# The second MLP product of two of four token chunks in seven block products of eight

## The chip, the core and the metric

The kernel runs on one core of a Trainium2 chip. The metric is the time of one execution on the device in microseconds (us). Five engines work side by side, each through its own list of instructions in a fixed order: TensorE (PE, with its weight loads as PEld), VectorE (DVE), ScalarE (ACT), GpSimd (POOL) and SyncE (SP), which issues nearly all DMAs. They wait for each other through semaphores.

## What is computed

The reference is a trunk of two layers for 1024 tokens of width 1024. What matters here is the MLP at each layer's end, with 4096 inner columns:

```python
def sq_relu_mlp(h, w1, w2):
    a = jax.nn.relu(h @ w1)
    return (a * a) @ w2
...
        h = rms_norm(x, mlp_norm_g[layer])
        x = x + sq_relu_mlp(h, mlp_w1[layer], mlp_w2[layer])
    return rms_norm(x, final_g)
```

Everything is float32.

## The kernel before

The tokens are worked on in two chunks of 512 (x[0] and x[1], each four row blocks of 128 tokens times two column halves of 512). So there are four MLPs: a0 (layer 0, first chunk), b0 (layer 0, second chunk), a1 and b1 (layer 1). In the program they stand in the order a0, b0, a1, b1; the convolution module of layer 1 is woven into b0 and a1, and a0 and b1 run nearly alone. Names in the profile carry the chunk's letter (m_a, o_b), not the layer.

PE multiplies float32 in a form that rounds, so each operand is split in a high and a low part, and each product takes three matmuls: low times high (L157), high times low (L158) and high times high (L159), all 128x128 by 128x512. The high part is made by a cast on ACT, the low part by a subtraction on DVE; for the weights these are wh and wl, made from a loaded tile raw (L104 and L105 for w2, L125 and L126 for w1), 1024 columns at a time.

`mlp` (L243) works on 32 inner tiles of 128 columns. m1(f) multiplies the normed chunk hT by a column tile of w1 in 24 matmuls into a PSUM bank (tag m1, two banks), takes relu to r (L252), squares r twice on ACT, once cast into the high part ah (L254) and once in place (L255), and subtracts for the low part al (L256). m2(g, h) takes four inner tiles (G = 4) and one column half of w2: for each of four row blocks 12 matmuls into a PSUM bank o (tag mm, four banks), and an addition into x on DVE (L240). A list sets the order in which the program is written: the first m1 of the next group stands ahead of the two m2 of a group:

```python
            n = (g + 1) * G
            order += [(m1, n)] if n < NF else []
            order += [(m2, g, 0), (m2, g, 1)]
            order += [(m1, f) for f in range(n + 1, min(n + G, NF))]
```

From what is written a scheduler sets, when the program is built, the order on each engine; at run time it is fixed. Tiles come from pools with a number of buffers for each tag: 48 of [128, 512] in pool hp (x, the normed chunk, and others), four wh and four wl of [128, 1024], two raw. The norm ahead of an MLP (`norm_parts`) squares and sums x on ACT, scales it on DVE, transposes it on PE into the bank pair tr, and makes hh (ACT) and hl (DVE). In a0 the norm of x[1], named m, stands behind the first steps of a0. `finish` does the last norm and the output.

Of the kernel before, what the change touches and what calls it, by code (L numbers as in the profile page):

```python
# [31 lines left out]
def tile_hybrid_trunk(  # L32
# [7 lines left out]
    nc = tc.nc  # L40
# [5 lines left out]
    lp = ctx.enter_context(tc.tile_pool(name="lp", bufs=8))  # L46
# [8 lines left out]
    def hf(name):  # L55
        return ht(name, F32)
# [10 lines left out]
    def m1_ps(name):  # L67
        return mmp[0].tile([P, C], F32, tag="m1", bufs=2, name=name)
# [203 lines left out]
    NG = FF // (G * P)  # L272


    w_in = ev_w_in[0]
    y = [[None] * KT for _ in range(NCH)]
    dp = ctx.enter_context(tc.tile_pool(name="dp", bufs=1, space=bass.MemoryType.DRAM))
    with tc.tile_pool(name="p1", bufs=1) as p1, tc.tile_pool(name="ps1", bufs=1, space=PSUM) as ps1:
        mmp = (ps1, 2)

        def qt(name):
            return p1.tile([P, C], F32R, tag="q", bufs=8, name=name)
# [314 lines left out]
        for h in range(NH):  # L597
            out_proj((1,), 1, h)

    p2 = ctx.enter_context(tc.tile_pool(name="p2", bufs=1))  # L600
    p2.tile([P, 96], F32, tag="pad", bufs=1, name="pad_p2")
    ps2 = ctx.enter_context(tc.tile_pool(name="ps2", bufs=1, space=PSUM))
    mmp = (ps2, 4)

    def bt(name, dt=F32):
        return p2.tile([P, C], dt, tag="b", bufs=11, name=name)

    def ct(name):
        return p2.tile([P, C], F32, tag="c", bufs=9, name=name)


    halo = cp.tile([P, KT, HALO], F32, name="halo")
# [89 lines left out]
        rows_into_x(s[kg * 4:kg * 4 + 4], ws, h, x[c], f"q2{c}{kg}{h}")  # L702

    def finish(c):
        fg = [ct(f"fg{c}{h}") for h in range(NH)]
        for h in range(NH):
            nc.sync.dma_start(fg[h], final_g[h * C:(h + 1) * C].rearrange("(a d) -> a d", a=1).to_broadcast((P, C)))
        for t in range(TT):
            o = [ct(f"fo{c}{t}{h}") for h in range(NH)]
# [24 lines left out]
    steps(a0)  # L734
    b0 = mlp(0, hm[1], x[1], "b0")
    steps(b0, -1)
    h1a = norm(x[0], "od_g", 0, ct, "oa")
# [56 lines left out]
```

## Time and profile before

| what | us |
|---|---|
| median of 3 runs (lowest, highest) | 2218.25 (2216.99, 2218.44) |
| the profiled execution | 2218.34 |
| its span in the trace | 2216.5 |
| PE busy | 2176.4 (98%) |
| DVE busy | 1411.7 (64%) |
| ACT busy | 954.7 (43%) |
| POOL busy | 113.0 (5%) |

The profile is of one execution. Matmuls overlap: each is recorded with about 390 ns, while the next starts some 0.23 us after it, so the starts tell the pace. The granted clock, the share of TensorE's full 2.4 GHz that the chip allows, is 0.997 in the mean. The matmuls of a0 lie between about 518 and 859 us, those of b1 between 1860.7 and 2208.9 us.

### The profile page before, as it was taken

To read this page: it belongs to the slowest core of one execution; us is meant where nothing else is said; L and a number is where in the kernel's file an instruction comes from. 1 tells how busy PE (TensorE), PEld (TensorE's weight loads), DVE (VectorE), ACT (ScalarE), POOL (GpSimd) and SP (SyncE) were. 2 spreads that over 40 slices of the span, in tenths; PEclk is the share of its full clock that TensorE was granted. 3 is DMA by queue.
4 is the path that set the end of the run, shared out by engine and by line. 5 is a ranking of instruction groups with operands and counts; after the bars stand their busy time and mean duration, and the time that the engine had idled before them with its cause. 6 is when DMAs were issued, how large, how long until landed. Compare 5 with 4: busy or idle time off the path is not lost.

```text
span 2216.5 us, 25970 instructions
## 1 busy us (share of the span) xinstructions
PE 2176.4 (98%) x10180; PEld 1768.2 (80%) x10180; DVE 1411.7 (64%) x1934; ACT 954.7 (43%) x1509; POOL 113.0 (5%) x296
## 2 busy tenths in 40 slices
PE   7999999899999999999999999999999999999998
PEld 5867776678888888888888888788888888888887
DVE  4377878856433444579899664999886555444344
ACT  4466677535333334433333362443333545333332
POOL 1000000000000001100000010300000001000000
PEclk9999999999999999999999999999999999999999
DMA  4111013022323223332222323222222224222232
GB/s 160 57 34 43 34 53 127 35 73 67 109 95 95 96 95 100 100 95 95 95 96 96 95 95 96 86 96 95 95 96 95 95 97 147 99 95 95 95 95 76
DMA packets 172010, 199.25 MB, mean 90 GB/s; under 512 B 5648, under 2 KB 120688, under 8 KB 171888
## 3 DMA queue, kind: packets, MB, share of 16 engines
q1 hardware_dynamic: 171872, 197.59, 27.5%
q8 instruction: 80, 1.31, 0.2%
q14 instruction: 42, 0.34, 0.1%
q10 hardware_dynamic: 16, 0.00, 0.0%
HBM read 190.23 MB, written 7.34 MB: 89 GB/s over the span
## 4 chain that ended last, share of the span: by engine, by line
PE 94%; DVE 3%; ACT 1%; DMA 1%; issue 1%; POOL 0%; SPq 0%; DVEq 0%; POOLq 0%; ACTq 0%
PE m_a L157 5%; PE m_a L158 5%; PE m_b L159 5%; PE m_a L159 5%; PE o_a L158 5%; PE o_a L159 5%; PE m_b L157 5%; PE o_a L157 5%; PE m_b L158 5%; PE o_b L159 5%; PE o_b L157 5%; PE o_b L158 5%; PE av L529 2%; PE xg L158 1%; PE wt L521 1%; PE xg L157 1%
## 5 line engine op out<-in xcount | busy, mean ns | idle before, releaser
L648 DVE SCALAR_TENSOR_TENSOR cv<-u,dwT,cv 128x512 f32<-128x512 f32 x480 | 340.3, 756 | 0.2
L157 PE MATMUL o_a<-wh_w2a,al_a 128*128 128x512 f32 x512 | 199.6, 390 | 0.0
L158 PE MATMUL o_a<-wl_w2a,ah_a 128*128 128x512 f32 x512 | 199.5, 390 | 0.0
L157 PE MATMUL o_b<-wh_w2b,al_b 128*128 128x512 f32 x512 | 199.4, 390 | 0.0
L159 PE MATMUL o_b<-wh_w2b,ah_b 128*128 128x512 f32 x512 | 199.4, 389 | 0.0
L158 PE MATMUL o_b<-wl_w2b,ah_b 128*128 128x512 f32 x512 | 199.3, 389 | 0.0
L159 PE MATMUL o_a<-wh_w2a,ah_a 128*128 128x512 f32 x512 | 198.9, 389 | 0.0
L125 ACT CAST wh_w1b<-raw_w1b 128x1024 fp32r<-128x1024 f32 x64 | 67.4, 1053 | 211.8 <-PE o_b L159 168.5
L105 DVE TENSOR_TENSOR wl_w2a<-raw_w2a,wh_w2a 128x1024 fp32r<-128x1024 f32 x64 | 78.3, 1224 | 121.9 <-ACT wh_w2a L104 121.9
L125 ACT CAST wh_w1a<-raw_w1a 128x1024 fp32r<-128x1024 f32 x64 | 67.4, 1054 | 205.2 <-PE o_a L159 169.7
L105 DVE TENSOR_TENSOR wl_w2b<-raw_w2b,wh_w2b 128x1024 fp32r<-128x1024 f32 x64 | 80.3, 1254 | 116.0 <-ACT wh_w2b L104 116.0
L240 DVE TENSOR_TENSOR xr<-o_a,xr 128x512 f32<-128x512 f32 x128 | 87.5, 687 | 75.9 <-PE o_a L159 75.7
L240 DVE TENSOR_TENSOR xr<-o_b,xr 128x512 f32<-128x512 f32 x128 | 87.9, 687 | 71.3 <-PE o_b L159 70.9
L158 PEld LDWEIGHTS o_b<-wl_w2b,ah_b 128*128 128x128 f32 x512 | 96.1, 188 | 19.9
L157 PEld LDWEIGHTS o_a<-wh_w2a,al_a 128*128 128x128 f32 x512 | 96.1, 188 | 19.9
L159 PEld LDWEIGHTS o_b<-wh_w2b,ah_b 128*128 128x128 f32 x512 | 96.1, 188 | 19.8
L159 PEld LDWEIGHTS o_a<-wh_w2a,ah_a 128*128 128x128 f32 x512 | 96.1, 188 | 19.8
L157 PEld LDWEIGHTS o_b<-wh_w2b,al_b 128*128 128x128 f32 x512 | 96.1, 188 | 19.7
L158 PEld LDWEIGHTS o_a<-wl_w2a,ah_a 128*128 128x128 f32 x512 | 96.2, 188 | 19.7
L252 ACT ACTIVATE r_b<-m_b 128x512 f32<-128x512 f32 x64 | 38.3, 599 | 169.6 <-PE m_b L159 169.6
L252 ACT ACTIVATE r_a<-m_a 128x512 f32<-128x512 f32 x64 | 38.3, 598 | 163.0 <-PE m_a L159 163.0
L126 DVE TENSOR_TENSOR wl_w1b<-raw_w1b,wh_w1b 128x1024 fp32r<-128x1024 f32 x64 | 77.9, 1220 | 36.1 <-ACT wh_w1b L125 35.7
(537 smaller groups left out, 5345.0 us busy)
## 6 DMA issues: line engine op xcount, KB each, us to landing
raw_w1a<-in_mlp_w_dram SPq DMA_DIRECT2D x32, 1024.0 KB, 5.1
raw_w2a<-in_mlp_w_dram SPq DMA_DIRECT2D x32, 1024.0 KB, 5.0
raw_w1b<-in_mlp_w_dram SPq DMA_DIRECT2D x32, 1024.0 KB, 5.1
raw_w2b<-in_mlp_w_dram SPq DMA_DIRECT2D x32, 1024.0 KB, 4.9
raw_pw<-in_od_pw_w_dram SPq DMA_DIRECT2D x32, 512.0 KB, 4.5
raw_q<-in_od_pw_w_dram SPq DMA_DIRECT2D x8, 1024.0 KB, 4.9
raw_wo<-in_ev_w_out_dram SPq DMA_DIRECT2D x6, 768.0 KB, 4.9
xa<-in_x_dram SPq DMA_DIRECT2D x16, 256.0 KB, 5.1
```

The source lines that it names most:

```text
L105: paced(V.tensor_tensor(lo, raw, hi.bitcast(F32), op=ALU.subtract), 1)
L125: A.copy(hi, srcs[i])
L126: paced(V.tensor_tensor(lo, srcs[i], hi.bitcast(F32), op=ALU.subtract), 2)
L157: T.matmul(acc, ll, rh, start=(i == 0), stop=False)
L158: T.matmul(acc, lh, rl, start=False, stop=False)
L159: T.matmul(acc, lh, rh, start=False, stop=(i == n - 1))
L240: paced(V.tensor_tensor(xt[t][h], acc, xt[t][h], op=ALU.add), 1.5)
L252: A.activation(r, acc, AF.Relu)
L521: T.transpose(pt[:, b * P:(b + 1) * P], ke[:, b * P:(b + 1) * P], ident)
L529: ins = T.matmul(av[j * 64:j * 64 + 64, tt * P:(tt + 1) * P], vt[lo_s // P + b][:, hc:hc + 64], wts[j][:, b * P:(b + 1) * P], start=(diag ...
L648: waiting.append(lambda k=k, m=m: V.scalar_tensor_tensor(cv[m], u[m][:, k:k + C], dwT[:, k * KT + m:k * KT + m + 1], cv[m], op0=ALU.mult, ...
```

## The change

a0 and b1 are no longer made by `mlp` but by a new function, `mlp7`, in four groups of eight inner tiles; b0 and a1 stay. For the second product it takes the activations as a 2x2 matrix of blocks (rows: the chunk's first and last 256 tokens; columns: even and odd inner tiles), and w2 so too (even and odd inner rows, left and right column half). Strassen's algorithm in Winograd's form gives the product of two such matrices with seven block products in place of eight, from sums of blocks: of activations s1 to s4, of weights t1 to t4. Each block product is 2 row blocks x 4 inner tiles x 3 = 24 matmuls, 168 in a group, where eight made 192.

- A pair of inner tiles is made by `pair`: two m1 (24 matmuls each, as before), relu (L298) and one square (L299), the sums s1 to s4 of 256 columns on DVE (L301 to L305), and the high (L292, ACT) and low parts (L293, DVE) of all seven blocks, in two tiles sh and sl of 1792 columns.
- The weights are loaded as single [128, 512] tiles by SP (L315). The tile w11 is changed in place: an accumulating DMA from GpSimd's queue adds w12 to it, which makes t1 (L323), DVE adds w22 for t2 (L367) and w21 for t4 (L381); t3 is w12 with w22 added by DMA. Each stage is split into wh and wl (L332, L333), 512 columns at a time, in the four buffers each that were there.
- The products run in the order w11, t1, t2, w22, t3, w21, t4, into two bank pairs: pa, and pb (later pc). Some go on accumulating in a bank that was read before. After a product DVE adds the banks into x, or subtracts them (L347), 14 times in a group.
- Four pairs come first, then the seven products; the next group's m1 stand behind them in the program.
- The norm of x[1] is spread over the products of a0's last group. The pools of banks and of b0's and a1's tiles are closed and opened around the two new calls, and `finish` takes its tiles from hp.

```diff
+    def mlp7(layer, hT, xt, name, pa, psa, within=None):
+        def pair(f, n):
+            un = col_units(w1, f * P, (f + 1) * P, f"w1{n}")
+            lo = pa.tile([P, 7 * B2], F32R, tag="sl", bufs=4, name=f"sl{n}")
+            hi = pa.tile([P, 7 * B2], F32R, tag="sh", bufs=4, name=f"sh{n}")
+            ev, od, sa, sb = [hf(f"r{i}_{n}") for i in range(4)]
+            (a21, a11), (a22, a12), (s1, s3), (s2, s4) = [(r[:, :B2], r[:, B2:]) for r in (ev, od, sa, sb)]
+            def parts(r, s0):
+                sl = slice(s0 * B2, s0 * B2 + r.shape[1])
+                A.copy(hi[:, sl], r)
+                V.tensor_tensor(lo[:, sl], r, hi[:, sl].bitcast(F32), op=ALU.subtract)
+            for i, r in enumerate((ev, od)):
+                acc = m1_ps(f"m1_{n}{i}")
+                colmm(acc, un(i), hT)
+                A.activation(r, acc, AF.Relu)
+                A.activation(r, r, AF.Square)
+                if i == 0:
+                    V.tensor_tensor(s3, a11, a21, op=ALU.subtract)
+                    parts(a11, 0)
+            V.tensor_tensor(s1, a21, a22, op=ALU.subtract)
+            V.tensor_tensor(s2, s1, a11, op=ALU.subtract)
+            V.tensor_tensor(s4, a12, s2, op=ALU.add)
+            for r, s0 in ((od, 1), (sa, 3), (sb, 5)):
+                parts(r, s0)
+            return hi, lo
...
+        def w_add(ts, g, odd, h):
+            for k in range(4):
+                f = 8 * g + 2 * k + odd
+                Q.dma_start(ts[k], w2[f * P:(f + 1) * P, h * C:(h + 1) * C], accum_op=ALU.add)
...
+                for row, h, op in into:
+                    x_ = xt[(2 if row == 1 else 0) + t][h]
+                    V.tensor_tensor(x_, x_, banks[t], op=op)
...
+            acts = [pair(8 * g + 2 * p, f"{n}{p}") for p in range(4)]
...
+            ba, bb = bank(f"pa_{n}", "sa"), bank(f"pb_{n}", "sb")
+            t1 = w_rows(g, 0, 0, "w11")
+            product(ba, acts, 0, w_split(t1, f"w11{n}"), True, [(1, 0, ALU.add)])
+            w_add(t1, g, 0, 1)
+            w22 = w_rows(g, 1, 1, "w22")
+            product(bb, acts, 3, w_split(t1, f"t1{n}"), True, [(2, 1, ALU.add)])
+            for k in range(4):
+                V.tensor_tensor(t1[k], t1[k], w22[k], op=ALU.add)
+            product(ba, acts, 5, w_split(t1, f"t2{n}"), False, [(1, 1, ALU.subtract)])
+            others()
+            product(bb, acts, 6, w_split(w22, f"w22{n}"), False, [(1, 1, ALU.add)])
...
+            t3 = w_rows(g, 0, 1, "w12")
+            w_add(t3, g, 1, 1)
+            product(ba, acts, 4, w_split(t3, f"t3{n}"), False, [(2, 1, ALU.subtract)])
...
+            bc = bank(f"pc_{n}", "sb")
+            product(bc, acts, 2, w_split(w21, f"w21{n}"), True, [(1, 0, ALU.add)])
...
-    a0 = mlp(0, hm[0], x[0], "a0")
-    steps(a0, -1)
-    hm[1] = norm(x[1], "mlp_g", 0, ct, "m1")
-    steps(a0)
+    hm[1] = []
+    strassen(0, hm[0], x[0], "a0", norm_parts(x[1], "mlp_g", 0, hf, "m1", TT, hm[1]))
...
-    b1 = mlp(1, h2b, x[1], "b1")
-    steps(b1)
+    mid.close()
+    strassen(1, h2b, x[1], "b1")
```

On ACT, in the kernel before, the rows around a group's last m1 in the middle of b1 read so (r the relu's output, m the m1 bank, wh_w2 the high part of w2 for the second product):

```order
L252 ACTIVATE r_b_14632<-m_b_14603 128x512
L254 ACTIVATE ah_b_14634<-r_b_14632 128x512
L255 ACTIVATE r_b_14632<-r_b_14632 128x512
L104 CAST wh_w2b_14745<-raw_w2b_14743 128x1024
L252 ACTIVATE r_b_14670<-m_b_14641 128x512
L104 CAST wh_w2b_14749<-raw_w2b_14743 128x1024
L254 ACTIVATE ah_b_14672<-r_b_14670 128x512
L255 ACTIVATE r_b_14670<-r_b_14670 128x512
```

The casts of w2 stand between the relus of the m1 tiles. In the changed kernel ACT's rows at the step from the second group's last pair to its first product are these (r 15765 is od, r 15766 holds s1 and s3, r 15767 s2 and s4):

```order
L298 ACTIVATE r_b_15765<-m_b_15802 128x512
L299 ACTIVATE r_b_15765<-r_b_15765 128x512
L292 CAST shb_15763<-r_b_15765 128x512
L292 CAST shb_15763<-r_b_15766 128x512
L292 CAST shb_15763<-r_b_15767 128x512
L332 CAST wh_w11b_15854<-w11b_15846 128x512
L332 CAST wh_w11b_15854<-w11b_15848 128x512
L332 CAST wh_w11b_15860<-w11b_15850 128x512
L332 CAST wh_w11b_15860<-w11b_15852 128x512
L332 CAST wh_t1b_15904<-w11b_15846 128x512
```

All casts of the weights w11 now stand behind the last pair's relu, square and casts.

On DVE, in the kernel before, the additions into x (xr) stand in b1 between splits for the next products, and the bank o that an addition reads is one of four:

```order
L105 TENSOR_TENSOR wl_w2b_14746<-raw_w2b_14743,wh_w2b_14745 128x1024
L105 TENSOR_TENSOR wl_w2b_14750<-raw_w2b_14743,wh_w2b_14749 128x1024
L240 TENSOR_TENSOR xr_3895<-o_b_14687,xr_3895 128x512
L256 TENSOR_TENSOR al_b_14673<-r_b_14670,ah_b_14672 128x512
L240 TENSOR_TENSOR xr_3899<-o_b_14701,xr_3899 128x512
L240 TENSOR_TENSOR xr_3903<-o_b_14715,xr_3903 128x512
```

In the changed kernel DVE's rows of the same group from the last split of w11 on begin with these (pa is the bank pair of product 1; w11 15846 is the first of the four tiles that turn into t1, t2 and t4):

```order
L333 TENSOR_TENSOR wl_w11b_15861<-w11b_15852,wh_w11b_15860 128x512
L333 TENSOR_TENSOR wl_t1b_15905<-w11b_15846,wh_t1b_15904 128x512
L347 TENSOR_TENSOR xr_3903<-xr_3903,pa_b_15842 128x512
L367 TENSOR_TENSOR w11b_15846<-w11b_15846,w22b_15896 128x512
L347 TENSOR_TENSOR xr_3907<-xr_3907,pa_b_15843 128x512
L333 TENSOR_TENSOR wl_t1b_15905<-w11b_15848,wh_t1b_15904 128x512
```

and 13 rows later they reach the bank pair pb of product 2, which product 4 (w22) goes on with:

```order
L333 TENSOR_TENSOR wl_w22b_15991<-w22b_15900,wh_w22b_15990 128x512
L333 TENSOR_TENSOR wl_w22b_15991<-w22b_15902,wh_w22b_15990 128x512
L367 TENSOR_TENSOR w11b_15852<-w11b_15852,w22b_15902 128x512
L347 TENSOR_TENSOR xr_3896<-xr_3896,pb_b_15844 128x512
L347 TENSOR_TENSOR xr_3900<-xr_3900,pb_b_15845 128x512
L333 TENSOR_TENSOR wl_t3b_16035<-w12b_16022,wh_t3b_16034 128x512
```

From the first addition of pa to the first of pb, both counted, these are 20 instructions. The order is the same in seven of the eight groups; in a0's last one the rows of the norm stand between.

## Rows read from the trace of the kernel before

**Rows 1.** Page, part 1: busy us (share of the span) and instructions by engine.

```profile
PE 2176.4 (98%) x10180; PEld 1768.2 (80%) x10180; DVE 1411.7 (64%) x1934; ACT 954.7 (43%) x1509; POOL 113.0 (5%) x296
```

**Rows 2.** Windows inside a0 and b1; columns as the first line says, instructions in brackets.

```profile
core 0: us, PE busy (x) PEld busy (x) DVE busy (x) ACT busy (x) POOL busy (x), PEclk, DMA share, GB/s
500.00:800.00 300.00, 299.10 (x1350) 248.08 (x1349) 132.56 (x160) 115.95 (x165) 4.69 (x12) 1.00 0.28 92
1900.00:2200.00 300.00, 300.00 (x1325) 248.51 (x1324) 120.22 (x138) 102.64 (x137) 0.00 (x0) 1.00 0.28 92
```

**Rows 3.** Timeline in b1: start, duration, engine, line, instruction [idle before, releaser].

```profile
1995.57 1.05 ACT L125 CAST wh_w1b<-raw_w1b 128x1024 fp32r<-128x1024 f32 x1 [8.46 <-PE o_b L159]
1996.66 1.22 DVE L126 TENSOR_TENSOR wl_w1b<-raw_w1b,wh_w1b 128x1024 fp32r<-128x1024 f32 x1 [1.75 <-ACT wh_w1b L125]
...
2001.95 0.39 PE L159 MATMUL m_b<-hh_mb,wh_w1b 128*128 128x512 f32 x1
2002.17 0.39 PE L157 MATMUL m_b<-hh_mb,wl_w1b 128*128 128x512 f32 x1
2002.37 0.60 ACT L252 ACTIVATE r_b<-m_b 128x512 f32<-128x512 f32 x1 [4.38 <-PE m_b L159]
```

**Rows 4.** Instructions by line and shape, whole span: count | busy us, mean ns | idle before.

```profile
L252 ACT ACTIVATE r_b<-m_b 128x512 f32<-128x512 f32 x64 | 38.3, 599 | 169.6 <-PE m_b L159 169.6
L254 ACT ACTIVATE ah_b<-r_b 128x512 fp32r<-128x512 f32 x64 | 40.3, 630 | 0.6
L256 DVE TENSOR_TENSOR al_a<-r_a,ah_a 128x512 fp32r<-128x512 f32 x64 | 44.0, 688 | 28.4 <-ACT r_a L255 28.4
L240 DVE TENSOR_TENSOR xr<-o_b,xr 128x512 f32<-128x512 f32 x128 | 87.9, 687 | 71.3 <-PE o_b L159 70.9
L517 DVE TENSOR_TENSOR ke<-z,ke 128x256 f32<-128x256 f32 x16 | 6.5, 419 | 1.0
```

**Rows 5.** Timeline ahead of a0: ACT and DVE busy back to back at 128x512.

```profile
378.95 0.63 ACT L167 CAST y01h<-yr 128x512 fp32r<-128x512 f32 x1
379.46 0.65 ACT L423 ACTIVATE xc<-xgt 128x512 f32<-128x512 f32 x1
...
381.10 0.68 DVE L168 TENSOR_TENSOR y01l<-yr,y01h 128x512 fp32r<-128x512 f32 x1
...
381.70 0.69 DVE L424 SCALAR_TENSOR_TENSOR xc<-xc,xgt 128x512 f32<-128x512 f32 x1
...
382.30 0.69 DVE L168 TENSOR_TENSOR y11l<-yr,y11h 128x512 fp32r<-128x512 f32 x1
```

**Rows 6.** DMA issues: count, KB each, median us from issue to landing.

```profile
xa<-in_x_dram SPq DMA_DIRECT2D x16, 256.0 KB, 5.1
...
out_dram<-fo SPq DMA_DIRECT2D x16, 256.0 KB, 2.0
yr<-yd SPq DMA_DIRECT2D x12, 256.0 KB, 3.0
```

**Rows 7.** Timeline of PE behind a long wait, early in the kernel.

```profile
122.23 0.33 PE L498 MATMUL z<-ks,q 128*128 128x128 f32 x1 [3.62 <-DVE ks L564]
...
124.07 0.63 PE L159 MATMUL xg<-hh_e,wh_xg 128*128 128x512 f32 x1
124.49 0.63 PE L157 MATMUL xg<-hh_e,wl_xg 128*128 128x512 f32 x1
```

**Rows 8.** Windows, columns as in rows 2: the granted clock behind two waits of PE.

```profile
120.00:125.00 5.00, 2.77 (x11) 2.29 (x12) 4.88 (x7) 4.93 (x10) 0.00 (x0) 0.77 0.02 3
125.00:130.00 5.00, 5.00 (x21) 3.92 (x19) 4.97 (x8) 2.08 (x6) 0.00 (x0) 0.89 0.70 210
...
1425.00:1430.00 5.00, 2.37 (x13) 1.73 (x12) 5.00 (x6) 0.00 (x0) 0.95 (x1) 1.00 0.00 0
```

**Rows 9.** Waits of PE, whole span: total us, times, longest us.

```profile
PE nps_ma L214 <- DVE hl_ma L220: 2.9, 2, 2.6
```

**Rows 10.** Instructions by line: the Square pass of the norm of x[1].

```profile
L186 ACT ACTIVATE xn_m<-xr 128x512 f32<-128x512 f32 x16 | 10.0, 626 | 10.5 <-DVE xr L240 10.5
```

More of the change, by code (lines that the diff above doesn't have):

```diff
@@ L272, in tile_hybrid_trunk, with w_rows, w_split, product @@
     NG = FF // (G * P)
+    B2 = 2 * P
+    def mlp7(layer, hT, xt, name, pa, psa, within=None):
+        w1, w2 = mlp_w1[layer], mlp_w2[layer]
+        def pair(f, n):
[22 more added lines that the diff above has]
+            return hi, lo
+        def w_rows(g, odd, h, nm):
+            ts = []
+            for k in range(4):
+                f = 8 * g + 2 * k + odd
+                t_ = hf(f"{nm}{name}{g}{k}")
+                nc.sync.dma_start(t_, w2[f * P:(f + 1) * P, h * C:(h + 1) * C])
+                ts.append(t_)
+            return ts
+        def w_add(ts, g, odd, h):
+            for k in range(4):
+                f = 8 * g + 2 * k + odd
+                Q.dma_start(ts[k], w2[f * P:(f + 1) * P, h * C:(h + 1) * C], accum_op=ALU.add)
+        def w_split(ts, nm):
+            res = []
+            for i in range(2):
+                hi = wp.tile([P, 1024], F32R, tag="wh", bufs=4, name=f"wh_{nm}{i}")
+                lo = wp.tile([P, 1024], F32R, tag="wl", bufs=4, name=f"wl_{nm}{i}")
+                for j in range(2):
+                    js = slice(j * C, (j + 1) * C)
+                    A.copy(hi[:, js], ts[2 * i + j])
+                    V.tensor_tensor(lo[:, js], ts[2 * i + j], hi[:, js].bitcast(F32), op=ALU.subtract)
+                    res.append((hi[:, js], lo[:, js]))
+            return res
+        def product(banks, acts, slot, ws, first, into):
+            for t in range(2):
+                ts = slice(slot * B2 + t * P, slot * B2 + (t + 1) * P)
+                for i, ((hi, lo), (rh, rl)) in enumerate(zip(acts, ws)):
+                    T.matmul(banks[t], lo[:, ts], rh, start=(first and i == 0), stop=False, skip_group_check=not first)
+                    T.matmul(banks[t], hi[:, ts], rl, start=False, stop=False, skip_group_check=not first)
+                    T.matmul(banks[t], hi[:, ts], rh, start=False, stop=(i == 3), skip_group_check=not first)
+                for row, h, op in into:
+                    x_ = xt[(2 if row == 1 else 0) + t][h]
+                    V.tensor_tensor(x_, x_, banks[t], op=op)
+        def bank(nm, tag):
+            return [psa.tile([P, C], F32, tag=tag, bufs=2, name=f"{nm}{t}") for t in range(2)]
+        for g in range(FF // (8 * P)):
+            n = f"{name}{g}"
+            acts = [pair(8 * g + 2 * p, f"{n}{p}") for p in range(4)]
+            more = within if g == FF // (8 * P) - 1 and within is not None else iter(())
+            def others():
+                for _ in range(3):
+                    next(more, None)
+            ba, bb = bank(f"pa_{n}", "sa"), bank(f"pb_{n}", "sb")
[4 more added lines that the diff above has]
+            product(bb, acts, 3, w_split(t1, f"t1{n}"), True, [(2, 1, ALU.add)])
+            for k in range(4):
+                V.tensor_tensor(t1[k], t1[k], w22[k], op=ALU.add)
+            product(ba, acts, 5, w_split(t1, f"t2{n}"), False, [(1, 1, ALU.subtract)])
+            others()
+            product(bb, acts, 6, w_split(w22, f"w22{n}"), False, [(1, 1, ALU.add)])
+            others()
+            t3 = w_rows(g, 0, 1, "w12")
+            w_add(t3, g, 1, 1)
+            product(ba, acts, 4, w_split(t3, f"t3{n}"), False, [(2, 1, ALU.subtract)])
+            others()
+            w21 = w_rows(g, 1, 0, "w21")
+            bc = bank(f"pc_{n}", "sb")
+            product(bc, acts, 2, w_split(w21, f"w21{n}"), True, [(1, 0, ALU.add)])
+            others()
+            for k in range(4):
+                V.tensor_tensor(t1[k], t1[k], w21[k], op=ALU.add)
+            product(ba, acts, 1, w_split(t1, f"t4{n}"), False, [(2, 0, ALU.add)])
+            for _ in more:
+                pass
@@ L277, in tile_hybrid_trunk @@
     dp = ctx.enter_context(tc.tile_pool(name="dp", bufs=1, space=bass.MemoryType.DRAM))
[L278 removed]
+    lpp = [None]
+    with tc.tile_pool(name="lp1", bufs=1) as lp1, tc.tile_pool(name="p1", bufs=1) as p1, \
+            tc.tile_pool(name="ps1", bufs=1, space=PSUM) as ps1:
         mmp = (ps1, 2)
+        lpp[0] = lp1
         def qt(name):
@@ L704, in finish @@
     def finish(c):
-        fg = [ct(f"fg{c}{h}") for h in range(NH)]
+        fg = [hf(f"fg{c}{h}") for h in range(NH)]
         for h in range(NH):
@@ L708, in finish @@
         for t in range(TT):
-            o = [ct(f"fo{c}{t}{h}") for h in range(NH)]
+            o = [hf(f"fo{c}{t}{h}") for h in range(NH)]
             rs = rstd_of(x[c][t], o[0], f"f{c}{t}")
```

23 lines of the change are left out of this document (15 added, 8 removed).

## The prediction

> **What bounds the kernel now.** I read the page's busy shares first, then the windows over the two MLPs that the change touches, then single instructions in the timeline. PE is busy for 98% of the span [rows 1]. In the stretches inside a0 and b1 it is busy for 299.10 and 300.00 of 300 us at a granted clock of 1.00, while DVE works 44% and 40%, ACT 39% and 34% of them [rows 2]. So there the time is the number of matmuls times PE's pace, 300 / 1325 = 0.2264 us each, and everything else is hidden, because the weights of a block are cast and split long before PE comes to it. Work taken from PE is worth its full time, if PE then still never waits.
>
> **What it removes.** A group of eight inner tiles now has 7 x 24 = 168 matmuls in its second product, where it had 192. Eight groups (a00 to a03, b10 to b13) lose 8 x 24 = 192, and 192 x 0.2264 = **43.5 us**, 5.43 per group. Nothing comes back on PE: the operand sums are made by DVE and by accumulating DMAs, and the result is added from PSUM by DVE.
>
> **What it adds per group.** All of it is on ACT, DVE and DMA: 28 casts and 28 subtractions 128x512 for the split of the summed weights, 8 additions of weights, 14 additions into x (before: 16), four short sums and a wider hi/lo split per pair, 8 accumulating DMAs on GpSimd's queue. In all DVE has about 50 instructions of 0.60 us in a product phase of 168 x 0.2264 = 38.0 us: 30 us, which fits by the sum. The cost is therefore not in the amount but in the order, and I walked through one group with it. The steps come from these rows: PE's result is seen by ACT 0.20 us after the slot behind the last matmul (2002.17 to 2002.37), a hand-over from ACT to DVE takes 0.04 (1995.57 + 1.05 to 1996.66) [rows 3]; relu 0.60, square 0.63, a DVE 128x512 0.69, 128x256 0.42 [rows 4]; on one engine the next 128x512 starts 0.51 later on ACT and 0.60 later on DVE [rows 5]. Casts 128x512 I take at the 0.62 to 0.63 of those rows. Time 0 is the slot in which PE could issue the first product's first matmul.
>
> **Hold 1, the weights behind the last pair.** ACT's order (the first two fences) has the first cast of w11 behind relu, square and all three casts of the last pair, where before a 1024-wide cast of w2 stood between the relus. Relu 0.20 to 0.80, square to 1.47, cast of od to 2.15. The third cast needs s4, and s4 stands on DVE behind s1 (from 1.55), s2 and the low part of od (2.36 to 2.96): it ends at 3.37. Cast of (s2, s4) from 3.42, first cast of w11 from 3.93 to 4.55, PE starts at 4.59. Before, the same place cost nothing. Cover: none, since m1 of the next group now stands behind the products. Without the detour over DVE the chain on ACT alone (0.20 + 0.60 + 0.63 + two hand-overs + three casts at 0.51 + 0.62 for w11 + a hand-over) gives 3.7; 3.7 to 4.6 are its bounds. I keep **4.6**.
>
> **Hold 2, the low part.** DVE makes wl of w11 behind the low part of (s2, s4), from 4.68 to 5.37; PE has only two matmuls to do until then (4.59 + 0.45 = 5.04): **0.4**. Product 1 ends at 10.4.
>
> **Hold 3 and 4, DVE's queue ahead of bank pb.** This is the third fence. After four subtractions for w11 (until 7.1) DVE waits for the first cast of t1 = w11 + w12, and this for an accumulating DMA, issued once 5.37 has freed the tile. No row shows an accumulating DMA or any DMA from GpSimd's queue. The nearest rows, 256 KB each, take 2.0 (out), 3.0 (yr) and 5.1 us (xa, at the start, beside others) [rows 6]; I take 3.0, the row that reads from DRAM without a crowd, and keep 2 to 8 for the range (8 as twice the middle of 3.0 and 5.1). By the Trainium skill, "DMA: Bandwidth & Descriptors", section on the anatomy of one DMA, a transfer issued by GpSimd costs about 2.0 us and its bytes at 436 GB/s, an estimate of 2.6 us for 256 KB; no run here shows it, and with it the sum would stay the same, since up to 3.0 the landing is not what comes last. It lands at 8.4, DVE continues at 9.1, and then the addition of bank pa into x stands in its queue and waits for the end of product 1's first bank, 10.2. From there 20 instructions stand up to the addition of bank pb that frees it: 10.2 + 20 x 0.60 = 22.2, with hand-overs 22.4. PE has 42 matmuls to do between product 1 and the first of w22 on bank pb: 10.4 + 42 x 0.2264 = 19.9, and loses **0.5** on the way (hold 3, last part of t1); it comes at 20.4 and waits **2.0** (hold 4). Behind it wl of t3 is late by **0.6**, then PE is ahead no longer and the rest is hidden.
>
> The Trainium skill, "Perfetto Trace Analysis", section "Optimizing Tensor Performance", says that independent matmul groups should rotate through different PSUM banks, so that the evacuation of one overlaps the next. The row for DVE's pace decides what that is worth here: with a third pair of banks hold 4 would be gone, and a group would lose 2.0 less; with two pairs it speaks against this order.
>
> **The sum of a group** is 4.6 + 0.4 + 0.5 + 2.0 + 0.6 = 8.1 us lost against 5.43 saved. Bounds: with DVE at 0.55 a step and no hand-over 6.5, at 0.65 9.1; with the landing at 4, 5.1, 6.5 and 8 us 8.5, 9.6, 11.0 and 12.5; with hold 1 alone 3.7 to 4.6.
>
> **The clock.** Where PE waited 3.62 us, its matmuls then came 0.42 apart (124.07, 124.49) [rows 7], the pace of 1.2 GHz, and the two stretches of 5 us show 0.77 and 0.89: (0.23 + 0.11) x 5 = 1.7 us lost [rows 8]. Behind a wait of 2.6 us [rows 9] the stretch, from 1425, has 1.00 [rows 8]. Hold 1 is longer than both, so I expect the drop in each group: 1.7, of which 0.4 lies in hold 2, so **+1.3**. A group then loses 9.4.
>
> **Group a03.** The norm of x[1], which stood at the start of a0, is now spread over a03's products. Its 8 Square passes on ACT at 0.626 us [rows 10] with their accumulator reads are 5.6 us, and some five of them stand in ACT's queue ahead of the first cast of t1, which is wanted there: **+3.4** (0 if they fell in idle time, 6 with DVE's 16 instructions on the path too). PE's 32 transposes are only moved.
>
> **Edits at nothing.** The second square gone, fg and fo in other tiles, the reopened pools: they lie beside PE work of 300 of 300 us [rows 2]; uncovered, a new pool's first use could wait about 1 us twice. Between a0 and b1 PE's, ACT's and DVE's order is the same.
>
> **Sum.** The profiled execution took 2218.34, the median 2218.25, so no correction. 2218.3 - 43.5 + 7 x 9.4 + (9.4 + 3.4) = **2253**. Without the clock's drop: 2218.3 - 43.5 + 7 x 8.1 + 11.5 = 2243.
>
> **Rivals.**
> A. As above, with the drop 0.42 (2253, by DVE's pace and landing 2246 to 2262) or without it 0.25 (2243, 2233 to 2250). For the drop speaks [rows 7], against it that only one such wait is shown there.
> B. The accumulating DMAs land late, 8 us or more after their issue: GpSimd's queue has not carried one, four follow each other, and in a0 w21's loads run beside them. 12.5 a group: 2218.3 - 43.5 + 8 x 12.5 + 3.4 = 2278. For it speaks the 5.1 of xa [rows 6], against it DRAM traffic of only 92 GB/s [rows 2]. 0.15.
> C. The other side: DVE's queue does not bind. If DVE's steps are shorter than 0.60 where it never waits, or PE, coming 4.6 us later, leaves it that lead, the pb addition comes in time, and only hold 1 stays, 3.7 to 4.6, in the middle 4.1. 8 x 4.1 + 3.4 = 36, against 43.5: 2211 (2207 to 2220). It decides at 5.0 us a group. Against it stand 20 instructions on one queue and [rows 5]. 0.15, of which a third within 0.2%.
> D. The change doesn't do what it says, that is, hold 1 vanishes too and 2175 is reached: it would need ACT's order to be another; 0.03.
>
> **How the numbers follow.** A with the drop is likeliest: 2253. The range leaves out D, the lower half of C and the upper half of B: 2216 to 2275. Within 0.2% (4.4 us, about what a measurement of this kernel can tell from no change) lies a third of C and the edge of A's lower bound, 0.06; faster 0.13; slower 0.81.
>
> **What would show it.** In the profile after: PE rows 192 fewer; at each of eight places a wait of PE of 4 to 5 us on the cast of w11, with the clock below 1.00 behind it; a second wait of about 2 us of the first w22 matmul on DVE's addition of pb into x; DVE near 80% in the product phase; GpSimd's DMAs landing in about 3 us. Wrong would be: no wait on pb (C), or waits of ACT on those DMAs that end last (B).

## The result, and the profile after

The changed kernel took 2272.94 us (median of 4 runs, 2272.03 to 2276.2) against 2218.09 before: slower by a ratio of 1.0249, 95% interval [1.0234, 1.0264]. The forecast was 2253 within 2216 to 2275: the sign was right and the range held, but 35 us were forecast and 55 came. The profiled execution took 2272.03 us, its span is 2270.0.

The page of the changed kernel answers [rows 1]: 192 PE instructions fewer, as counted, and PE busy for 95% where it was 98%.

```profile
PE 2166.0 (95%) x9988; PEld 1743.1 (77%) x9988; DVE 1577.2 (69%) x2334; ACT 1045.1 (46%) x1733; POOL 171.1 (8%) x360
```

PE's longest waits in a0 and its waits in b1, where there were none to speak of [rows 2]. Columns: waiting engine, tile and line, what was waited for, us in total, times, longest. First those of a0 (518 to 900 us), then, after the dots, those of b1 (1870 to 2270):

```profile
PE pa_a L342 <- ACT wh_w11a L332: 13.1, 3, 4.4
PE pb_a L342 <- DVE xr L347: 5.3, 3, 1.8
PE pa_a L342 <- issue: 4.4, 1, 4.4
PE nps_m L213 <- DVE xn_m L208: 2.9, 1, 2.9
...
PE pa_b L342 <- ACT wh_w11b L332: 13.1, 3, 4.4
PE pb_b L342 <- DVE xr L347: 6.9, 4, 1.7
PE pa_b L342 <- issue: 4.4, 1, 4.4
PE pa_b L342 <- DVE xr L347: 1.5, 4, 0.4
PE pb_b L343 <- DVE wl_t1b L333: 0.6, 2, 0.3
```

Eight times 4.4 us at the first matmul of product 1 is hold 1 (the row "issue" is the same place in each MLP's first group). The waits on the addition of pb into x are hold 4, seven times; between the first addition of pa and that of pb DVE has 20 instructions in b1's first two groups, 19 in five others (one addition of weights stands ahead of pa's there) and 14 in a0's last.

Rows picked out of one group, the first of b1, in the timeline (start, duration, engine, line, instruction, [idle before, releaser]); its last m1 matmul starts at 1933.96, so time 0 of the prediction's walk is 1934.19:

```profile
1934.38 0.60 ACT L298 ACTIVATE r_b<-m_b 128x512 f32<-128x512 f32 x1 [3.73 <-PE m_b L158]
1938.05 2.17 ACT L332 CAST wh_w11b<-w11b 128x512 fp32r<-128x512 f32 x4
1938.77 1.19 PE L342 MATMUL pa_b<-wh_w11b,slb 128*128 128x512 f32 x2 [4.42 <-issue]
1939.76 0.63 PE L343 MATMUL pa_b<-wl_w11b,shb 128*128 128x512 f32 x1
1939.78 3.63 POOL L323 DMA_DIRECT2D w11b<-in_mlp_w_dram  x4 [43.19 <-DVE wl_w11b L333]
1940.18 0.63 PE L344 MATMUL pa_b<-wh_w11b,shb 128*128 128x512 f32 x1
1942.28 4.67 POOL L323 DMA_DIRECT2D w12b<-in_mlp_w_dram  x4
1944.07 0.62 ACT L332 CAST wh_t1b<-w11b 128x512 fp32r<-128x512 f32 x1 [3.84 <-DMA w11b<-in_mlp_w_dram]
1946.46 1.29 DVE L347 TENSOR_TENSOR xr<-xr,pa_b 128x512 f32<-128x512 f32 x2 [1.04 <-PE pa_b L344]
1958.02 1.28 DVE L347 TENSOR_TENSOR xr<-xr,pb_b 128x512 f32<-128x512 f32 x2
1958.76 0.50 PE L342 MATMUL pb_b<-wh_w22b,slb 128*128 128x512 f32 x1 [1.74 <-DVE xr L347]
```

Read against the walk: the first cast of w11 was to start at 3.93 and starts at 3.86, PE was to start at 4.59 and starts at 4.58. The matmuls of product 1 then come 0.42 apart (1939.76 to 1940.18), the half level, for the first twelve. The first addition of pa starts at 1946.46, that of pb 11.6 us later, which is 19 steps of 0.60. What is not as the walk had it is the DMA: the cast of t1 waits 3.84 us for it, and does not run until 9.88 on the walk's clock, where 8.4 stood. Yet it is not what comes last here: DVE, done with that tile's low part, waits another 1.04 us for the end of product 1, which the slow matmuls have put off, before it can add pa. In b1's four groups this idle time is 0.5 to 1.3 us.

The accumulating DMAs of b1 (KB each, median us from issue to landing), the row that was missing from [rows 6], with a plain load of the same size for comparison. The median hides a spread: the first of the four into w11 lands 3.9 to 5.8 us after its issue in the eight groups, the fourth 5.7 to 8.8.

```profile
w11b<-in_mlp_w_dram SPq DMA_DIRECT2D x16, 256.0 KB, 5.8
...
w11b<-in_mlp_w_dram POOLq DMA_DIRECT2D x16, 256.0 KB, 6.6
w12b<-in_mlp_w_dram POOLq DMA_DIRECT2D x16, 256.0 KB, 9.3
```

Where the time went, from the starts of PE's matmuls. A group is counted from its first m1 matmul to the next group's; 360 matmuls at 0.2264 are 81.5 us of it.

| term | forecast, us | measured, us |
|---|---|---|
| 192 matmuls fewer | -43.5 | -43.5 |
| lost in seven groups | 7 x 9.4 = 66 | 72.8 (91.1 to 92.8 a group) |
| lost in a03, its transposes taken out | 12.8 | 20.4 |
| behind the last matmul | 0 | +4.3 (11.9 for 7.6) |
| elsewhere | 0 | -0.5 |
| sum of the spans | +35 | +53.5 |

### The profile page after: what moved, and what is told of

Its sections match the earlier page's. It is cut to its first block, busy times and chain, and to the rows that moved or that the text cites. A ratio compares the mean times of both kernels' runs of the same rounds, so it can differ in the third digit from the quotient of the medians.

```text
span 2270.0 us, 26589 instructions
## 1 busy us (share of the span) xinstructions
PE 2166.0 (95%) x9988; PEld 1743.1 (77%) x9988; DVE 1577.2 (69%) x2334; ACT 1045.1 (46%) x1733; POOL 171.1 (8%) x360
## 4 chain that ended last, share of the span: by engine, by line
PE 83%; DVE 7%; issue 5%; ACT 3%; DMA 2%; POOL 0%; SPq 0%; POOLq 0%; DVEq 0%; ACTq 0%
PE m_b L156 5%; PE m_b L158 5%; PE m_b L157 5%; PE m_a L156 4%; PE m_a L158 4%; PE m_a L157 4%; PE o_b L157 3%; PE o_a L158 3%; PE o_a L156 3%; PE o_b L156 3%; PE o_a L157 3%; PE o_b L158 3%; PE av L644 2%; DMA w11a<-in_mlp_w_dram 2%; PE xg L157 1%
## 5 line engine op out<-in xcount | busy, mean ns | idle before, releaser
L156 PE MATMUL m_b<-hh_m,wl_w1b 128*128 128x512 f32 x256 | 100.0, 391 | 1.6 <-DVE xr L347 1.6
L156 PE MATMUL m_b<-hh_mb,wl_w1b 128*128 128x512 f32 x256 | 99.7, 389 | 0.8 <-DVE xr L239 0.8
L156 PE MATMUL m_a<-hh_ma,wl_w1a 128*128 128x512 f32 x256 | 100.3, 392 | 0.0
L158 PE MATMUL m_b<-hh_m,wh_w1b 128*128 128x512 f32 x256 | 100.1, 391 | 0.0
L156 PE MATMUL o_a<-wh_w2a,al_a 128*128 128x512 f32 x256 | 100.0, 391 | 0.0
L157 PE MATMUL m_a<-hl_ma,wh_w1a 128*128 128x512 f32 x256 | 99.9, 390 | 0.0
L158 PE MATMUL m_a<-hh_ma,wh_w1a 128*128 128x512 f32 x256 | 99.9, 390 | 0.0
L158 PE MATMUL o_b<-wh_w2b,ah_b 128*128 128x512 f32 x256 | 99.8, 390 | 0.0
L157 PE MATMUL o_a<-wl_w2a,ah_a 128*128 128x512 f32 x256 | 99.8, 390 | 0.0
L157 PE MATMUL m_b<-hl_m,wh_w1b 128*128 128x512 f32 x256 | 99.8, 390 | 0.0
```

Source lines behind the costliest of these rows:

```text
L156: T.matmul(acc, ll, rh, start=(i == 0), stop=False)
L157: T.matmul(acc, lh, rl, start=False, stop=False)
L158: T.matmul(acc, lh, rh, start=False, stop=(i == n - 1))
```

## The experiments

**Only b1.** a0 stays with `mlp` and its norm where it was, b1 is made by `mlp7`:

```diff
-    hm[1] = []
-    strassen(0, hm[0], x[0], "a0", norm_parts(x[1], "mlp_g", 0, hf, "m1", TT, hm[1]))
...
+    a0 = mlp(0, hm[0], x[0], "a0")
+    steps(a0, -1)
+    hm[1] = norm(x[1], "mlp_g", 0, ct, "m1")
+    steps(a0)
```

> Only the second half of the change: b1 in seven products, a0 as before, its norm of x[1] where it was. By the account of the two traces b1 loses 41.3 us in waits and low clock against 21.7 saved, and the end of the kernel behind its last matmul is 4.3 us longer: 2218 + 24 = 2242 us. Then a0 with the norm inside its last group costs the other 31. If the pools closed and opened again between the MLPs cost much, which the account doesn't have: more than 2246 here.

Measured 2241.95 us (ratio 1.0107, [1.0092, 1.0122]), as the account had it. So b1 costs 24 us and a0 31, and the pools that are closed and opened again cost no more than the account holds: 0.8 us of wait ahead of b1's first m1, here as in the change.

**Is the low clock on the path?** Twenty matmuls without use fill hold 1:

```diff
+            warm = tr_ps(f"warm_{n}")
+            for i in range(20):
+                T.matmul(warm, acts[3][0][:, :P], hT[i % KT][0], start=True, stop=True)
```

> One addition: 20 matmuls 128x512 without use between each group's last pair and product 1, into a bank that is idle there, 20 x 0.2264 = 4.5 us, so PE works through the time in which it waited 4.4 us for the cast of w11. Nothing else is moved. If the slow matmuls of product 1 (12 of them 0.19 us too late) come from that wait: clock back to about 0.997, product 1 takes 5.4 us in place of 7.9, 1 to 2.1 us won per group (the first, if the split of t1 is late then), 2256 to 2265 us. If the low clock has another cause: 2273 and 0.984 as before. If the accumulating DMAs set the pace of the products: clock back, but the same time, 2270 to 2273, with the waits on t1 longer by what product 1 is shorter.

Measured 2273.18 us (ratio 1.0247, [1.0232, 1.0263]), no change, though the clock rose to 0.990. The longest of PE's waits in the products say where the gain went:

```profile
PE pb_b L342 <- DVE xr L347: 7.2, 4, 1.8
PE pb_a L342 <- DVE xr L347: 5.3, 3, 1.8
PE pb_a L342 <- ACT wh_t1a L332: 4.2, 5, 2.5
PE pb_b L343 <- DVE wl_t1b L333: 4.0, 4, 1.1
...
PE pb_a L343 <- DVE wl_t1a L333: 1.5, 3, 0.9
```

Product 1 is faster, by 13 us over the eight groups, and product 2 waits for t1 instead: 9.7 us on the last three lines, where all waits on t1 in the change were 1.9 us (1.3 in a0, 0.6 in b1). In three groups the clock also falls a second time, behind the wait on pb; in the change it does so in one. That is near the third case of the expectation, not the first. The chain of work that ended last shows it (start, us, what): first the change in a0's first group, where it goes over an accumulating DMA, and in b1's first, where it goes over product 1's slow matmuls; then this run in b1's first group:

```profile
566.24 5.03 DMA w11a<-in_mlp_w_dram
...
1946.19 0.24 PE pa_b L344
1946.46 0.49 DVE xr L347
...
1944.15 5.83 DMA w11b<-in_mlp_w_dram
```

The change has the first form in all of a0's groups and the second in all of b1's; with the twenty matmuls it is a DMA into w11 in all eight. But the edit moved more than the clock: on DVE the scheduler has now put both additions of pa ahead of the first low part of t1, and DVE stands idle there (b1's first group: 3.12 us, until product 1 ends). So the run shows that filling this wait wins nothing here; it does not show what the low clock alone costs.

**Without the DMAs.**

```diff
-                Q.dma_start(ts[k], w2[f * P:(f + 1) * P, h * C:(h + 1) * C], accum_op=ALU.add)
+                pass
```

> Leaves out the 64 accumulating DMAs of GpSimd's queue, so that t1 is w11 and t3 is w12; everything else is there. Theory of order and clock: the wait on the cast of w11 (4.4) and the clock behind it stay, DVE's queue stays, only the waits on t1 go (0.6 a group, up to 1.0 in a0): 2264 to 2271 us. Rival, the DMAs landing after 6 to 9 us are what costs (my case B): 3 us or more a group go, 2249 or less.

Measured 2244.72 us (ratio 1.0121, [1.0106, 1.0136]): 28 us gone, so the rival is right and my theory of that moment falls. The groups of b1 take 88.7 us where they took 91.9, and of PE's waits in the products only hold 1 is left (8 times 4.4) and 0.4 us in a03. Holds 3 and 4 and the wait on t3 are not three causes. With the DMAs, the order that is written when the program is built has product 2's last part behind most of product 3, and ten splits on DVE between the additions of pa and of pb; without them it is another order, with none of these waits. So the 28 us are the landing and the order that is built around it, taken together; how they divide stays open.

**w11 ahead of the last pair.** First attempt at hold 1:

```diff
-            acts = [pair(8 * g + 2 * p, f"{n}{p}") for p in range(4)]
+            acts = [pair(8 * g + 2 * p, f"{n}{p}") for p in range(3)]
+            t1 = w_rows(g, 0, 0, "w11")
+            u1 = w_split(t1, f"w11{n}")
+            acts.append(pair(8 * g + 6, f"{n}3"))
```

> One change: the four tiles of w11 are loaded and split ahead of each group's last pair, in the wh and wl buffers that are there. Theory of order and clock: the wait of 4.6 us ahead of product 1 goes, and with it the low clock behind it (2.5 us), 7.1 us in each of eight groups, 57 in all: 2216 us, clock above 0.99, no wait of PE on the cast of w11 over 1 us. Rival, the next wait takes its place: DVE's queue ahead of the addition of bank pb is as long as before, and PE comes to it 7 us earlier; then the wait on that addition grows from 1.7 to 4 us or more and only 2 to 4 us a group are won: 2240 to 2257. Rival, the accumulating DMAs set the pace: they too start earlier here, so this run alone doesn't tell them apart.

Measured 2271.02 us (1.0236, [1.0219, 1.0253]): the wait did not go, it moved. In the timeline of this kernel PE waits as long as before for the same cast, now ahead of the last pair, because 18 of product 1's matmuls stand ahead of that pair's m1 in PE's order, and w11's casts behind the third pair's on ACT:

```profile
2021.10 1.66 ACT L332 CAST wh_w11b<-w11b 128x512 fp32r<-128x512 f32 x3
...
2021.77 1.22 PE L342 MATMUL pa_b<-wh_w11b,slb 128*128 128x512 f32 x2 [4.37 <-ACT wh_w11b L332]
```

So this run tests nothing of what it was made for; with the next one it shows that a split belongs into a time in which ACT is idle, not just earlier in the program.

**w11 between the last pair's two m1.** There ACT was idle for 3.73 us (the first row of the group above).

```diff
+            us = [un(i) for i in range(2)] if between else None
             for i, r in enumerate((ev, od)):
...
                     parts(a11, 0)
+                    if between:
+                        between()
...
+            t1, u1 = [], []
+
+            def w11():
+                t1.extend(w_rows(g, 0, 0, "w11"))
+                u1.extend(w_split(t1, f"w11{n}"))
+            acts = [pair(8 * g + 2 * p, f"{n}{p}", w11 if p == 3 else None) for p in range(4)]
```

> w11 is loaded and split between the two m1 of each group's last pair, where ACT was idle for 3.7 us (in the run before this edit only moved the wait one pair ahead: PE had w11's products in its order before the last pair, and waited 4.4 us for the same casts there). The accumulating DMAs, which start when w11's low parts are made, start some 6 us earlier too. Theory of now: hold 1 and then the DMAs are in series, 4.6 and what lies behind it; both go: 8 to 10 us in each of eight groups, 2272.9 - 8 x 8.5 = 2205 us (2193 to 2215), clock above 0.995. Rival, the DMAs still land late for product 2 (6 us after their issue, wanted 8 us after it, the third and fourth later): waits on t1 of 2 us or more a group, 2220 to 2235. Rival, DVE's queue: from the first addition of pa to that of pb it is 10 instructions here, where it was 20; were the queue alone the cause, hold 4 would shrink to below 1 us and the rest stay.

Measured 2205.28 us, as forecast, and now faster than the kernel before: ratio 0.9944, [0.9929, 0.9959]. From the timeline of b1's second group in this kernel, ACT casts w11 behind the relu of the pair's first m1, and PE goes from m1 to product 1 with no wait:

```profile
1987.17 1.66 ACT L335 CAST wh_w11b<-w11b 128x512 fp32r<-128x512 f32 x3
...
1990.80 0.62 PE L345 MATMUL pa_b<-wh_w11b,slb 128*128 128x512 f32 x2
```

All that PE waits for in b1 (1863 to 2200 us) is this, and, after the dots, the largest wait of a0 (515 to 872 us):

```profile
PE pa_b L345 <- DVE xr L350: 1.7, 4, 0.4
PE m_b L156 <- DVE xr L239: 0.8, 1, 0.8
PE pa_b L346 <- DVE wl_t2b L336: 0.6, 2, 0.3
PE pa_b L345 <- DVE wl_t1b L336: 0.4, 1, 0.4
...
PE pa_a L345 <- ACT wh_t2a L335: 4.5, 3, 2.0
```

The groups of b1 take 83.1 us, 1.6 above their matmuls. The DMAs into b1's w11 still take 5.5 us from issue to landing (median), but the first is issued 2.0 us ahead of product 1's first matmul, where it was 1.0 us behind it and that matmul itself 4.6 us late, and in b1 PE hardly waits behind them any more. In a0's first three groups it still does, 1.0 to 2.0 us each: the chain there goes over the fourth DMA, issued only 2.3 us behind product 1's first matmul, to the cast of t2. Hold 1 and the DMA chain were in series; one edit took both, 8.8 us a group in b1 and 5.5 to 9.1 in a0's first three.

**DVE adds in place of the DMAs.** w12 is loaded once as a plain tile; w11 late as in the change, and then with the edit above:

```diff
-            w_add(t1, g, 0, 1)
+            t3 = w_rows(g, 0, 1, "w12")
+            for k in range(4):
+                V.tensor_tensor(t1[k], t1[k], t3[k], op=ALU.add)
...
-            t3 = w_rows(g, 0, 1, "w12")
-            w_add(t3, g, 1, 1)
+            for k in range(4):
+                V.tensor_tensor(t3[k], t3[k], w22[k], op=ALU.add)
```

> w11 late as in the change, but no accumulating DMA: w12 is loaded once as a plain tile, and DVE adds it into w11 and w22 into it, 8 more DVE instructions of 0.60 us a group, 58 in a product phase. If the DMAs' landing is what the waits behind hold 1 come from: as without the DMAs and with all other work (2244.7), plus at most 1 us a group for DVE: 2245 to 2253 us; hold 1 of 4.4 us and the low clock stay, and the clock costs 2.5 us a group since nothing hides it. If DVE's amount of work is what binds (35 of 38 us): 2273 or more, with waits on DVE.

> The two edits together: w11 split between the last pair's two m1, and DVE's additions in place of the accumulating DMAs. If the DMAs still bind with w11 early: some 10 us or more below the run with w11 early alone. If not, the same or up to 1 us a group above it, since DVE has 8 more instructions: 2200 to 2215 us.

Measured 2253.80 us with w11 late (ratio 1.0162, [1.0147, 1.0177]), just above the first case: 19 us are won by doing the additions on the busier engine. The orders on PE and DVE are others here too, so this again prices the landing together with the order. With w11 early it is 2240.17 us (1.0102, [1.0085, 1.0119]), 35 us above the run with w11 early and the DMAs left in. That I had not expected. PE's two largest waits in the products of that run:

```profile
PE pb_a L346 <- DVE wl_t1a L336: 12.1, 10, 2.2
PE pb_b L346 <- DVE wl_t1b L336: 9.8, 6, 2.2
```

With w11 early the last pair's sums and low parts, the split of w11, four additions and the split of t1 all fall into the time between the last pair and product 2, and DVE, which does one after the other, reaches the first low part of t1 at 2015.18 in the group where PE could have used it at 2013.4. A low clock follows that wait. Here arithmetic that DVE need not do is worth the DMAs' latency; with w11 late it is not.

**The clock again, with other covers.** The twenty matmuls of above, put into the run with DVE's additions and into the run without the DMAs:

> DVE's additions in place of the accumulating DMAs, and the 20 matmuls without use between last pair and product 1. With the DMAs these matmuls brought the clock back and won nothing, since the DMAs' landing took the place. If that was the reason, the low clock is on the path once the DMAs are gone: 2253.8 - 8 x 2.2 = 2236 us (2233 to 2242), groups of 87.3 us where they are 89.5. If the clock costs nothing in itself, or DVE's additions take the place as the DMAs did: 2248 to 2254.

> Leaves out the accumulating DMAs (t1 is w11, t3 is w12) and has the 20 matmuls without use between last pair and product 1. Twice these matmuls brought the clock back and won nothing, with the DMAs and with DVE's additions in their place; each time waits on t1 and t2 took what product 1 gave. Without the DMAs and with w11 late, groups took 88.7 us: 81.6 of matmuls, 4.5 of hold 1 and 2.5 of slow matmuls, and no other wait. If the clock's price is real and was only covered: 2244.7 - 8 x 2.2 = 2227 us (2224 to 2232), groups of 86.5. If DVE's queue covers it here too: 2240 to 2245.

Measured 2255.03 us in the first (1.0166, [1.0152, 1.0179]), again no gain: groups of 89.5 us with and without, and in the place of product 1's slow matmuls stand waits for DVE's low parts:

```profile
PE pb_a L343 <- DVE wl_t1a L333: 3.7, 5, 1.7
PE pa_b L343 <- DVE wl_t2b L333: 3.0, 8, 0.6
PE pa_a L343 <- DVE wl_t2a L333: 2.3, 6, 0.6
PE pb_b L343 <- DVE wl_t1b L333: 2.3, 4, 0.6
```

Without DMAs and without additions it is 2232.30 us (1.0064, [1.005, 1.0078]) against 2244.72: groups of 87.1 for 88.7, 12.4 us in all, less than the 18 expected. So filling hold 1 is worth 1.6 us a group where PE has hardly another wait in the products, and nothing where something else comes late. In each of the three pairs of runs the twenty matmuls also moved DVE's order, so these are prices of clock and order together. For the change itself DVE's idle time ahead of pa's first addition is a bound: in b1's groups DVE was ready for pa 0.5 to 1.3 us before the slow matmuls had ended; in a0's, where the chain goes over the DMAs, no row shows that they cost anything.

**A third bank pair.** This tries the rule that the prediction weighed at hold 4.

```diff
+            third = within is None or g != FF // (8 * P) - 1
+            bd = [tr_ps(f"pd_{n}{t}") for t in range(2)] if third else bb
...
-            product(bb, acts, 6, w_split(w22, f"w22{n}"), False, [(1, 1, ALU.add)])
+            product(bd, acts, 6, w_split(w22, f"w22{n}"), third, [(1, 1, ALU.add)])
```

(And product 2's banks are added into x twice.)

> The change with a third bank pair for product 4 (w22), in the two banks that the norm's transposes leave free, in all groups but a0's last; for it DVE adds product 2's banks into x twice, 2 additions more a group. w11 and the DMAs are as in the change. If hold 4 is the read of bank pb alone (1.9 us in each of seven groups): 2272.9 - 7 x 1.9 = 2260 us, with no wait of PE on an addition of pb. If the late DMAs are behind it (product 2's last quarter comes late, and w22 has to wait for that in any bank): the wait moves to t1, t3 or the low parts, and the time stays: 2267 to 2274.

Measured 2265.49 us (1.0214, [1.02, 1.0228]), 7.4 us less than the change, about half of the 13 and between the two cases. The wait on pb is gone from PE's list, and a new one stands there, on the low part of w21, 11.6 us in all:

```profile
PE pc_b L343 <- DVE wl_w21b L333: 6.6, 4, 1.7
PE pc_a L343 <- DVE wl_w21a L333: 5.0, 3, 1.7
```

The Trainium skill ("Perfetto Trace Analysis", "Optimizing Tensor Performance") says that independent matmul groups should rotate through different PSUM banks. As far as the bank goes this run agrees: the waits of 1.7 to 1.8 us are gone. The queue of the engine that empties the banks then shows itself at a later product; here too PE's order is another (part of w21's product stands ahead of t3's).

**The norm and the end.** In the run with w11 early, a0's last group still took 97.3 us. A new generator, written for this, cuts the norm into steps: Square passes between the group's pairs, two of eight steps behind each of four products, and in the second run one behind each of six. Both take the complete row blocks first in the last norm:

```diff
-            def others():
-                for _ in range(3):
+            def others():
+                for _ in range(2):
                     next(more, None)
...
-    finish(1)
+    finish(1, (2, 3, 0, 1))
```

> The run with w11 early, with two more edits: the norm of x[1] in a0's last group is spread over it (Square passes between its pairs, two of its eight steps behind each of four products, the second half scaled early), and the last norm takes the row blocks that are complete first ahead of the others. a0's last group takes 97.3 us in the run with w11 early, of which 4.2 are the transposes and 81.6 the matmuls: 11.5 in waits and low clock. If these come from the norm in a lump: 6 to 9 us go there; the end of the kernel is 2 us shorter: 2205.3 - 9 = 2196 us (2191 to 2200). If DVE's amount of work in that group binds (50 instructions and the norm's 16, about 39 us against 42 of PE): 2201 to 2206.

> The run with the norm spread, with one of its eight steps behind each of the six first products in place of two behind each of four. In that run a0's last group still took 95.3 us: waits of 1.3, 1.2 and 2.5 us around the norm's last steps and t3, and low clock behind them. If spreading does it: 4 to 6 us there, 2196 us (2194 to 2199). If the order of ACT and DVE around t3 does it, which this moves little: 2199 to 2203.

Measured 2201.06 us (0.9926, [0.9912, 0.994]) and 2196.46 us (0.9907, [0.9894, 0.9921]). In the first, the end behind the last matmul is 7.9 us where it was 11.9 in the run with w11 early, all of it from the order of the row blocks, and a0's last group takes 95.3 us, 2 less where I expected 6 to 9: the norm's last steps still stood together ahead of t3, with a wait of 2.5 us on t3's low part and the low clock behind it. One step per product brings that group to 90.4 us, so it was the lump and not DVE's amount of work. This version beats the kernel before by 21.6 us, half of the 43.5 that the matmuls are worth.

## Why the prediction was right or wrong

**The matmuls** and **hold 1** were right: 192 fewer, and 4.58 us for 4.59. So was the reason given for hold 1, w11's casts behind the last pair's: putting them into ACT's idle time removes it.

**Hold 2** (0.4) is covered by the slow matmuls in the change, and appears as soon as these are gone: 0.35 us at the same matmul in all three runs with matmuls without use.

**The landing** was taken too short. I took 3.0 us from the row that reads without a crowd [rows 6] and kept 2 to 8 for the range. The term stands for the first of the four tiles, and its DMA landed after 3.9 to 5.8 us, 4.3 in the first group of b1; the medians of all are 6.2 and 6.6 us into w11 and 9.3 into w12. The estimate from the Trainium skill's fit ("DMA: Bandwidth & Descriptors", anatomy of one DMA), 2.6 us, is farther off still. By the prediction's own table 4 and 5.1 us gave 8.5 and 9.6 us a group, 9.8 and 10.9 with the clock's 1.3, where 10.4 were measured. But only in a0's groups does the chain go over the DMAs. Case B, 8 us or more and 12.5 a group, was not met; its sign, DMAs that end last, was there in a0 and not in b1. Without the DMAs 28 us go, but that is landing and order together, and the runs do not divide it. I gave B 0.15.

**Holds 3 and 4 and t3**, 0.5 + 2.0 + 0.6, measured in the first group of b1 with the slower matmul behind each: 0.6 + 2.0 + 0.65. The numbers were right, and the queue on DVE is the chain there as walked: from 1946.46 on 20 instructions follow each other about 0.60 apart. It is half of the cause: product 2 itself ends only at 1956.9 on PE, a microsecond before DVE gets to it, and with a third bank pair about half of hold 4 was won. Both orders are those that the scheduler built with the DMAs in the program; without them they are others.

**The clock** fell behind hold 1 in all eight groups, as forecast. In b1 it stayed low for longer: some twelve matmuls at 0.2 us too much, 2.5 to 3.0 us with hold 2, for 1.3 + 0.4. There it lies on the chain, and it is the term of a group that was mis-sized: 4.6 + 2.5 + 0.6 + 2.0 + 0.65 = 10.35 in b1's first group, for 9.4. In a0 it was 1.5 to 2.0 us, beside DMAs that came later still. That a0's groups too lost about 10.4 is partly luck: two errors of opposite sign met, a landing taken too short and a clock counted although it was covered.

**a03** lost 20.4 us, not 12.8. The Square passes that I priced at 3.4 us did little: between 845 and 860 us, where t1 is worked on, PE waits for nothing. What I left out is that the second half of the norm stands in PE's order as one block between w22 and t3, and waits there for DVE (2.9 and 1.4 us in the waits of PE) and t3 for ACT (1.3), with a second fall of the clock behind it. The windows of the changed kernel (us, PE, PEld, DVE, ACT, POOL busy, granted clock, DMA) show 0.71, 0.50 and 0.77, which is (0.29 + 0.50 + 0.23) x 5 = 5.1 us of lost pace, part of it in the waits:

```profile
870.00:875.00 5.00, 2.89 (x15) 2.15 (x16) 3.71 (x8) 1.46 (x3) 0.00 (x0) 0.71 0.44 117
875.00:880.00 5.00, 3.46 (x9) 2.06 (x9) 4.37 (x7) 4.83 (x10) 0.00 (x0) 0.50 0.00 0
880.00:885.00 5.00, 5.00 (x19) 4.03 (x18) 5.00 (x10) 1.64 (x3) 0.00 (x0) 0.77 0.02 5
```

**Edits at nothing** missed two. The reopened pools: b0's first m1 now waits 1.6 us and b1's 0.8 us for an addition on DVE, and before PE waited at neither place. The prediction named this, about 1 us twice, and left it at nothing (the 1.6 is within the 20.4 of a03). And the end: before, the last four additions into x came one by one, and the last norm followed them; now product 7 completes two row blocks at once, and three of four Square pairs run behind it on ACT. That is 4.3 us, and the order of the row blocks was worth 4.0 of it.

**The rivals.** C (DVE's queue does not bind) and D were not met. Slower, to which I gave 0.81, is what came. But 2273 lies above case A's 2262 and below B's 2278, in none of the cases as priced: about 7 us came from the seven groups, 7.6 from a03 and 4.3 from the end. The lower bounds of A do not follow from the prediction's own sums either: with DVE at 0.55 a step these give 2241 for 2246, and 2230 for 2233 without the drop.

## What to carry to other kernels

A saving on the busiest engine is worth what the hand-over between its phases leaves: look in the order for the first thing that the new phase needs, and for what stands ahead of it on the engine that makes it; here one split, moved into 3.7 us of idle time of another engine, turned a loss of 55 us into a gain of 13. Waits in series behind each other can't be priced one by one: fill or remove each in turn, and see whether the time moves or only the name of the wait, and whether the edit has moved the order on the engines too. A price that no row of the trace shows should set the width of the range towards its expensive side.

## What the runs showed of the hardware

An accumulating DMA moves about half of what a plain load does. Eight of them (2.1 MB) keep the 16 engines of the core busy at 134 to 216 GB/s, here from 1936 to 1955 us in steps of 0.475 us (the upper line is the busy share in tenths):

```profile
DMA  0000000000093799999899999999999999996100
GB/s 0 0 0 0 0 0 0 0 0 0 0 52 65 134 207 168 155 194 155 151 168 138 155 177 190 177 185 207 185 216 211 190 198 203 203 190 121 22 0 0
```

where the plain loads of the next group, of the same 256 KB each, from 2012 us on, run at about 400 at the same busy share (0.9 and more up to 2022, in steps of 0.475 us again):

```profile
GB/s 351 392 410 397 401 405 401 414 405 401 405 401 405 401 379 405 401 405 410 405 423 280 91 17 26 4 0 0 0 0 0 0 0 0 0 0 0 0 0 0
```

Of the eight accumulating DMAs the four into w12 queue behind the four into w11, and land 9.3 us after their issue (median).

Whether TensorE's clock falls behind a wait of 1.7 to 1.8 us does not follow from its length. Behind the wait ahead of w22 the matmuls came at full pace in six of the change's seven such groups (1.74 us in b1's first); in a0's second, behind 1.81 us, the half level followed (first two lines). In the run with the twenty matmuls two groups of b1 have nearly the same two waits, 1.07 and then 1.81 us in the third, 1.06 and then 1.81 us in the last: behind the third's the clock fell (third line), behind the last's it did not (fourth).

```profile
675.00:680.00 5.00, 3.91 (x12) 3.10 (x13) 4.13 (x7) 1.07 (x2) 0.00 (x0) 0.75 0.01 2
680.00:685.00 5.00, 4.82 (x20) 3.61 (x18) 1.75 (x3) 2.15 (x4) 0.00 (x0) 0.91 0.00 0
...
2145.00:2150.00 5.00, 5.00 (x15) 4.00 (x16) 3.04 (x5) 0.00 (x1) 0.00 (x0) 0.66 0.00 0
...
2239.00:2244.00 5.00, 5.00 (x24) 4.15 (x23) 2.52 (x5) 1.26 (x3) 0.00 (x0) 1.00 0.00 0
```

In the kernel before, 2.6 us had passed without it [rows 8, 9]. Behind the 4.4 us of hold 1 it fell each time, in eight groups of the change. What decides in between the runs do not settle.
